# Latent attention's rotary halves exchanged on VectorE, and its queries summed in half a bank

## The chip, the cores and the metric

The kernel runs on one core of one Trainium2 chip. The metric is the device time of one execution in microseconds (us); the figure of a kernel is the median of its runs. TensorE (PE in the profile, PEld for its weight loads) multiplies into PSUM banks of 128 rows by 512 float32 columns; VectorE (DVE) and ScalarE (ACT) read and write PSUM and SBUF; SyncE's queue (SP) issues nearly all transfers.

## The reference

Two layers over 256 tokens of width 2048, all in float32. A layer projects the normed input to differential attention (8 heads), multi-head latent attention (8 heads) and two gates, mixes both attentions through gates, and adds a SwiGLU block and a gated embedding. What matters here is how latent attention makes its queries and its shared key:

```python
qf = (rmsnorm(cq, g_q_latent[i]) @ w_q_up[i]).reshape(b, s, MLA_HEADS, 128 + 64)
q_nope = qf[..., :128]
q_rope = apply_rope(qf[..., 128:], cos_m, sin_m)
k_rope = apply_rope(kr[:, :, None, :], cos_m, sin_m)[:, :, 0, :]
scores = (q_nope . k_nope + q_rope . k_rope) * scale

def apply_rope(x, cos, sin):
    x1, x2 = jnp.split(x, 2, axis=-1)
    return concatenate([x1 * cos - x2 * sin, x2 * cos + x1 * sin])
```

The rotary part has 64 features, and feature d meets feature d + 32 (or d - 32). The latent `cq` has 512 features; the eight heads have 8 x 128 unrotated and 8 x 64 rotated query features. The order of the 64 features within query and key does not matter to the scores, as long as both have the same.

## The kernel before, in words

**Layout.** Activations stand with features on the 128 rows and the 256 tokens on the columns. Every matmul is a float32 product in parts: an operand u is kept as `[hi | lo]`, 512 columns, where `hi` is u rounded to a shorter type (fp32r) and `lo` the rest; a weight tile is split by `piece` into `hi` (ACT, L187) and `lo` (DVE, through the helper of L75) after its transfer by SP (L186). Weights come in pieces of up to eight 128 x 128 tiles; there are four buffers for arriving pieces and three each for `hi` and `lo`.

**A product.** `emit` makes two matmuls for each tile: weight `hi` by all 512 columns of u (L212), and weight `lo` by the 256 `hi` columns, added on the second half of the bank (L216). The result stands in two halves of a bank, and `joined` adds them: ACT copies the second half to SBUF (L242), DVE adds the first. There are four such banks (`ps_mm`). `product` does this for one output tile, `pair` for two tiles that share one piece.

**Latent queries and keys.** `queries_up(n)` takes a pair of tiles of `w_q_up`, each a product over the four tiles of `cq`. For n below 8 the tiles are unrotated queries: `joined`, then `split` into an operand. For n of 8 and 10 they are rotated queries, two heads of 64 features each on the 128 rows: `joined`, then `rotated`. `rotated` multiplies by a permutation matrix in float32 (`swap`, L367) to get each row's partner, and makes a * cos + partner * sin with three DVE instructions. The shared key (64 features, made once per layer by `narrow`) takes the same way with two matrices that also copy it to the other 64 rows: `halves` (L366) and `swaps` (L367). The three matrices and the frequencies come in one constant, `rope_c`, to the tile `rc`. For the differential heads, whose partners are 8 rows apart, `queries_keys` exchanges with `stream_shuffle` (L524), which permutes rows within each group of 32.

**Order.** `pipelined` walks the heads of an attention and between them steps a generator of other products: `beside` gives the differential attention its fill (keys, queries and keys of later heads, then `settle`, which norms the heads done, and the latent queries); the gate products fill the latent attention. The program is written in this order, and a scheduler with its own timing model then settles the order of the instructions on each engine for the whole kernel, except where the code pins it. Each engine works through its queue in order.

Of the kernel before, what the change touches and what calls it, by code (L numbers as in the profile page):

```python
# [16 lines left out]
ALU = mybir.AluOpType  # L17
AX = mybir.AxisListType

P = 128  # L20
T = 256
DM = 2048
NC = DM // P
DEPTH = 2
# [29 lines left out]
def encoder(ctx, tc, x, p, positions, cols, lams, wq, wk, wv, wcq, wckv, wkr, wga, wgb,  # L54
            w_q_up, w_kn, w_v, w_bd, w_bm, w_out, w_gate, w_up, w_down, w_pin, w_pg, rope_c, out):
    nc = tc.nc
    V, A, PE = nc.vector, nc.scalar, nc.tensor
# [10 lines left out]
    def scratch(tag, bufs, n=T):  # L68
        return tmp.tile([P, n], F32, tag=tag, name=tag, bufs=bufs)

    def bank(ps=ps_at, tag="at", name="at", shape=(P, 2 * T)):
        return ps.tile(list(shape), F32, tag=tag, name=name)

    def tt(o, a, b, op):
        return V.tensor_tensor(out=o, in0=a, in1=b, op=op)  # L75

    def stt(o, a, s, b, op0, op1):
        return V.scalar_tensor_tensor(out=o, in0=a, scalar=s, in1=b, op0=op0, op1=op1)
# [14 lines left out]
    def operand(t):  # L93
        return t.rearrange("p c t -> p (c t)")
# [4 lines left out]
    rc = const.tile([P, rope_c.shape[1]], F32, name="rc")  # L99
    nc.scalar.dma_start(gcol, cols)  # L100
    off = {}
    at = 0
# [13 lines left out]
    times = const.tile([P, 6], F32, name="times")  # L116
    for k in range(6):
        nc.gpsimd.memset(times[:, k : k + 1], 64.0 * 0.25 ** (k % 3) * (EPS if k > 2 else 1.0 / DM))
    swap, swaps, halves = (rc[:, 4 + j * P : 4 + (j + 1) * P] for j in range(3))
    aside = [fa(j) for j in range(5)]  # L120
    posi = aside[0][:, 0, :].bitcast(I32)
    posf = aside[0][:, 1, :]
# [86 lines left out]
    def emit(acc, hi, lo, at, us, first, last, inside=None):  # L209
        for j, u in enumerate(us):  # L210
            s, start, stop = slice((at + j) * P, (at + j + 1) * P), first and j == 0, last and j == len(us) - 1
            lead = PE.matmul(acc, hi[:, s], u, start=start, stop=False)  # L212
            if inside and inside[0] == j:
                with tc.issue_after(lead.ins):
                    inside[1]()
            rest = PE.matmul(acc[:, T:], lo[:, s], u[:, :T], start=False, stop=stop)  # L216
            if inside and inside[0] == j:
                tc.keep_in_program_order(rest)
# [9 lines left out]
            emit(acc, hi, lo, 0, us[a : a + m], a == 0, a + m == n, inside and (inside[0] - a, inside[1]))  # L228
        return acc

    def pair(src, us):

        n = len(us)
        hi, lo = piece(src.rearrange("n p m -> p n m"), 2 * n)
        for j in range(2):
            acc = bank(ps_mm, "mm", "mm")
            emit(acc, hi, lo, j * n, us, True, True)
            yield acc

    def joined(acc, o=None):  # L240
        t = scratch("join", 3)
        A.activation(t, acc[:, T:], AF.Copy)  # L242
        o = scratch("a", 4) if o is None else o
        tt(o, acc[:, :T], t, ALU.add)
        return o

    def split(u, src, gain=None):
        hi, lo = u[:, :T], u[:, T:]
        if gain is None:
            return A.activation(hi, src, AF.Copy), tt(lo, src, hi.bitcast(F32), ALU.subtract)  # L250
        return A.activation(hi, src, AF.Copy, scale=gain), stt(lo, src, gain, hi.bitcast(F32), ALU.mult, ALU.subtract)
# [91 lines left out]
    def stream(us, gain):  # L343

        acc = squares()

        def add(c):
            split(us[c], xT[:, c, :], g(gain, c))
            square_into(acc, xT[:, c, :], c == 0)

        return acc, add
# [9 lines left out]
        nc.gpsimd.memset(t.bitcast(F32), 0.0)  # L361

    def rotated(a, c_, s_, o=None):
        r = bank()
        if o is None:
            PE.matmul(r[:, T:], halves, a, start=True, stop=True)  # L366
        PE.matmul(r[:, :T], swap if o is not None else swaps, a, start=True, stop=True)  # L367
        t = scratch("sh", 2)
        tt(t, r[:, :T], s_, ALU.mult)
        tt(a, a if o is not None else r[:, T:], c_, ALU.mult)  # L370
        tt(a, a, t, ALU.add)
        if o is None:
            for j, t in enumerate(krs):
                split(t[64 * j : 64 * j + 64], a[64 * j : 64 * j + 64])
        else:
            split(o, a)
# [59 lines left out]
        return tmp.tile([P, 2, T], dt, tag=tag, name=tag, bufs=2)  # L436

    last_exp = [None]
    ROPE16 = [(j + 8) if j < 8 else (j - 8) if j < 16 else j for j in range(32)]

    def values(src, us, load=None):
# [43 lines left out]
    for L in range(DEPTH):  # L485

        steps = values(wv[L], ua, None if L else load)
        for vd in steps:
            if L == 0 and vd is not None:
# [3 lines left out]
                with after_splits():  # L493
# [5 lines left out]
                    cos_p, sin_p, cos_m, sin_m = tables()  # L499
# [20 lines left out]
        def queries_keys(h, *inside):  # L520
            for which, w in enumerate((wq, wk)):
                a = joined(product(w[L, h], ua, inside=(8, inside[which]) if inside else None))
                sh = scratch("sh", 2)
                V.stream_shuffle(sh, a, ROPE16)  # L524
                tt(sh, sh, sr, ALU.mult)
# [5 lines left out]
        cq, ckv = ub[8:12], ub[12:14]  # L531
        qn, kn, qr = [], [], ub[14:]
# [17 lines left out]
                split(kn[-1], joined(acc))  # L550

        def queries_up(n):
            for acc in pair(w_q_up[L, n : n + 2], cq):
                if n < MH:
                    qn.append(operand(fa(len(qn), F32R)))
                    split(qn[-1], joined(acc))
                else:
                    if n > MH:
                        qr.append(operand(fc(len(qr) - 2, F32R)))
                    at = qr[len(qr) - 1] if n > MH else qr[ropes[0]]  # L560
                    rotated(joined(acc), cos_m, sin_m, at)
                    ropes[0] += 1

        ropes = [0]
# [144 lines left out]
        acc, add = stream(ub, f"g_ffn{L}")  # L709
# [11 lines left out]
        for part, (f0, f1) in enumerate(FF_PARTS):  # L721
            for f in range(f0, f1):
                a = pre.pop(0) if pre else joined(product(w_gate[L, f], ub))
                tt(a, a, R, ALU.mult)
                s = scratch("sig", 2)
# [7 lines left out]
            if last:  # L733
                acc, add = stream(ub, f"g_ple{L}")
# [12 lines left out]
        if final:  # L747
            acc = squares()
# [5 lines left out]
        else:  # L754
            acc, add = stream(ua, f"g_mix{L + 1}")
        for n in range(NC - 2 * final):
            a = pre.pop(0) if pre else joined(product(w_pg[L, n], ub))
            tt(a, a, R, ALU.mult)
            s = scratch("sig", 2)
# [18 lines left out]
    for n in ends:  # L778
        parts[n] = [piece(w_pg[L, n][:, a * P : (a + PT) * P], PT) for a in (0, PT)]
        m = banks[n, 0] = bank(ps_mm, "mm", "mm")  # L780
# [7 lines left out]
    for n in ends:  # L788
        m = banks[n, 1] = bank(ps_mm, "mm", "mm")
        for j in range(whole[n], NC):  # L790
            w = slice(j % PT * P, (j % PT + 1) * P)
# [94 lines left out]
        ("g_q_latent0", 4), ("g_q_latent1", 4), ("g_kv_latent0", 2), ("g_kv_latent1", 2), ("g_subln", 2)]  # L886


def rope_constants():


    c = np.zeros((P, 4 + 3 * P), np.float32)
    f32 = np.float32
    for base, dim in ((0, 16), (2, 64)):
        inv = f32(THETA) ** (-np.arange(0, dim, 2, dtype=f32) / f32(dim))
        for q in range(P):
            d = q % 64
            if d < dim:
                c[q, base] = inv[d % (dim // 2)]
                c[q, base + 1] = -1.0 if d < dim // 2 else 1.0  # L900
    for q in range(P):
        c[q, 4 + (q ^ 32)] = 1.0
        for m in (q, q ^ 64):
            c[q, 4 + P + (m ^ 32)] = 1.0
            c[q, 4 + 2 * P + m] = 1.0
    return c


def tiles(w):

    d, k, n = w.shape
    w = w.reshape(d, k // P, P, n // P, P).transpose(0, 3, 2, 1, 4)
    return np.ascontiguousarray(w).reshape(d, n // P, P, k)
# [13 lines left out]
def laid_out(a):  # L927
    a = {k: np.asarray(v) for k, v in a.items()}
    w_in = a["w_in"]
    cut = np.cumsum([0, 1024, 1024, 1024, QR, KVR, 64, DM, DM])  # L930
    z = [w_in[:, :, cut[j] : cut[j + 1]] for j in range(8)]
    up = a["w_q_up"].reshape(DEPTH, QR, MH, 192)
    kv = a["w_kv_up"].reshape(DEPTH, KVR, MH, 256)
    flat = lambda w: w.reshape(w.shape[0], w.shape[1], -1)
    named = {f"{n}{i}": a[n][i] for n in ("g_mix", "g_ffn", "g_ple", "g_q_latent", "g_kv_latent") for i in range(DEPTH)}
    named["g_final"] = a["g_final"]
    named["g_subln"] = a["g_subln"]
    return {
        "x": np.ascontiguousarray(a["x"][0].T.reshape(NC, P, T).transpose(1, 0, 2)),
        "p": np.ascontiguousarray(a["p"][:, 0].transpose(0, 2, 1).reshape(DEPTH, 2, P, T).transpose(0, 2, 1, 3)),  # L940
        "positions": np.ascontiguousarray(a["positions"]),
        "cols": np.ascontiguousarray(np.concatenate([columns(named[n]) for n, _ in COLS], axis=1)),
        "lams": np.ascontiguousarray(np.stack([a["lambda_q1"], a["lambda_q2"], a["lambda_k1"], a["lambda_k2"]], axis=1).reshape(1, -1)),
        "wq": tiles(z[0]), "wk": tiles(z[1]), "wv": wide(z[2]), "wcq": tiles(z[3]), "wckv": tiles(z[4]),
        "wkr": np.ascontiguousarray(z[5].reshape(DEPTH, NC, P, 64).transpose(0, 2, 1, 3)).reshape(DEPTH, P, NC * 64), "wga": tiles(z[6]), "wgb": tiles(z[7]),
        "w_q_up": tiles(np.concatenate([flat(up[..., :128]), flat(up[..., 128:])], axis=2)),
        "w_kn": tiles(flat(kv[..., :128])), "w_v": wide(flat(kv[..., 128:])),
        "w_bd": tiles(a["w_branch_diff"]), "w_bm": tiles(a["w_branch_mla"]), "w_out": tiles(a["w_out"]),
        "w_gate": tiles(a["w_gate_up"][:, :, :DFF]), "w_up": tiles(a["w_gate_up"][:, :, DFF:]),
        "w_down": tiles(a["w_down"]), "w_pin": tiles(a["w_ple_in"]), "w_pg": tiles(a["w_ple_gate"]),  # L950
        "rope_c": rope_constants(),
    }
# [17 lines left out]
```

## Time and profile before

| | us |
|---|---|
| median of 3 runs | 2838.72 |
| lowest, highest | 2837.63, 2839.24 |
| the profiled execution | 2838.84 |
| its span in the profile | 2837.0 |

The granted TensorE clock was 0.999 of full speed over the span. Busy shares of the span: PE 100%, weight loads 88%, DVE 73%, ACT 54%. Durations of single matmuls in the profile overlap one another, so the distance between the starts of neighbours is the measure of what one costs. In rows of groups, `x` is the count and the two numbers behind the bar are busy us and mean ns; behind the second bar stands the idle time of the engine before them and what ended it. Tiles carry the program's names: `a` is a joined result, `at` a bank of the second pool, `mm` one of `ps_mm`, `sh` a scratch tile of the rotation. DVE's instructions are listed under the helpers L75 (two tensors), L78 and L81.

### The profile page before, as it was taken

Reading aid. Unit: us, or ns where it says so; the run is one execution under the profiler, and the core shown is the slowest. Engines: PE = TensorE matmul, PEld = TensorE weight load, DVE = VectorE, ACT = ScalarE, POOL = GpSimd, SP = SyncE. Lnnn points to the kernel's source line nnn. Section 1 sums busy time; section 2 is a strip of 40 time slices with the busy share of each in tenths; the row PEclk is TensorE's granted clock in tenths of the full one; section 3 lists DMA queues with packets and bytes.
Section 4 is the critical chain, followed back from the end, with each engine's and each line's share of the span. In section 5 each row is a group of like instructions: output and inputs, shape, how many; then the busy total and the mean of one; then the engine's idle time right before and its main releaser. Section 6 shows DMA issues by size and latency. Waiting matters only on the chain.

```text
span 2837.0 us, 44038 instructions
## 1 busy us (share of the span) xinstructions
PE 2826.8 (100%) x16743; PEld 2498.5 (88%) x16743; DVE 2073.0 (73%) x3537; ACT 1527.5 (54%) x2548; POOL 1.9 (0%) x15
## 2 busy tenths in 40 slices
PE   9999999999999999999999999999999999999998
PEld 7888888888888888888888888888888888888888
DVE  7997658776666766677869976687766666666777
ACT  6676545554444444455646755555544444444556
POOL 0000000000000000000000000000000000000000
PEclk9999999999999999999999999999999999999999
DMA  7544466666665566566665445666666656666664
GB/s 244 169 161 149 162 194 197 192 194 193 187 199 193 182 198 201 194 193 194 193 192 169 155 150 168 195 197 194 193 193 187 199 193 187 202 194 194 193 193 155
DMA packets 156596, 531.49 MB, mean 187 GB/s; under 512 B 16992, under 2 KB 24160, under 8 KB 156384
## 3 DMA queue, kind: packets, MB, share of 16 engines
q1 hardware_dynamic: 155952, 528.09, 58.9%
q8 instruction: 131, 2.15, 0.3%
q14 instruction: 81, 0.66, 0.1%
q10 hardware_dynamic: 432, 0.59, 0.1%
HBM read 526.52 MB, written 2.10 MB: 186 GB/s over the span
## 4 chain that ended last, share of the span: by engine, by line
PE 99%; DMA 1%; DVE 0%; ACT 0%; issue 0%; SPq 0%; DVEq 0%; ACTq 0%
PE mm L212 61%; PE mm L216 31%; PE S L406 1%; PE mmv L462 1%; PE mmv L460 1%; PE mmv L461 1%; DMA w<-in_wv 1%; PE at L424 1%; PE at L632 1%; PE at L689 0%; PE mm L776 0%; PE mm L392 0%; DVE wlo L75 0%; PE at L647 0%; DVE a L75 0%; PE at L367 0%
## 5 line engine op out<-in xcount | busy, mean ns | idle before, releaser
L187 ACT ACTIVATE whi<-w 128x1024 fp32r<-128x1024 f32 (+2 forms) x1030 | 1063.1, 1033 | 1241.4 <-issue 704.3
L75 DVE TENSOR_TENSOR wlo<-w,whi 128x1024 fp32r<-128x1024 f32 (+2 forms) x1030 | 1224.4, 1189 | 676.5 <-ACT whi L187 667.8
L212 PE MATMUL mm<-ub,whi 128*128 128x512 f32 x3936 | 1342.3, 390 | 0.3
L212 PE MATMUL mm<-ua,whi 128*128 128x512 f32 x3712 | 1271.4, 390 | 0.0
L216 PE MATMUL mm<-ub,wlo 128*128 128x256 f32 x3936 | 1085.1, 276 | 0.0
L216 PE MATMUL mm<-ua,wlo 128*128 128x256 f32 x3712 | 1027.3, 277 | 0.0
L212 PEld LDWEIGHTS mm<-ub,whi 128*128 128x128 f32 x3936 | 738.2, 188 | 153.1 <-DVE a L75 0.7
L212 PEld LDWEIGHTS mm<-ua,whi 128*128 128x128 f32 x3712 | 696.0, 188 | 142.0
L216 PEld LDWEIGHTS mm<-ub,wlo 128*128 128x128 f32 x3936 | 738.8, 188 | 1.1
L216 PEld LDWEIGHTS mm<-ua,wlo 128*128 128x128 f32 x3712 | 696.9, 188 | 2.4 <-DVE wlo L75 0.6
L75 DVE TENSOR_TENSOR a<-mm,join 128x256 f32<-128x256 f32 (+1 forms) x423 | 175.1, 416 | 1.6 <-ACT join L805 1.4
L242 ACT ACTIVATE join<-mm 128x256 f32<-128x256 f32 x452 | 166.5, 370 | 5.2 <-PE mm L216 4.8
L75 DVE TENSOR_TENSOR xT<-xT,mm 128x256 f32<-128x256 f32 x256 | 106.8, 420 | 41.5 <-PE mm L216 37.7
L75 DVE TENSOR_TENSOR a<-a,row 128x256 f32<-128x256 f32 (+1 forms) x209 | 87.5, 422 | 5.9
L75 DVE TENSOR_TENSOR a<-a 128x256 f32<-128x256 f32 x120 | 50.8, 425 | 4.0
L460 PE MATMUL mmv<-whi,ua 128*128 128x512 f32 x128 | 50.1, 395 | 1.7 <-ACT whi L187 1.7
L75 DVE TENSOR_TENSOR ua<-a,ua 128x256 fp32r<-128x256 f32 x120 | 49.9, 417 | 1.0 <-ACT ua L250 1.0
L461 PE MATMUL mmv<-whi,ua 128*128 128x512 f32 x128 | 49.6, 391 | 0.0
L250 ACT ACTIVATE ua<-a 128x256 fp32r<-128x256 f32 x120 | 48.2, 403 | 2.6 <-DVE a L75 2.6
L415 ACT ACTIVATE E<-S,nm 128x256 f32<-128x256 f32 x96 | 44.2, 472 | 2.1 <-DVE nm L81 2.0
L462 PE MATMUL mmv<-wlo,ua 128*128 128x512 f32 x128 | 43.8, 393 | 0.1
L75 DVE TENSOR_TENSOR ssq<-ssq,sq 128x256 f32<-128x256 f32 x96 | 40.1, 417 | 0.3 <-ACT sq L280 0.3
(195 smaller groups left out, 1209.8 us busy)
## 6 DMA issues: line engine op xcount, KB each, us to landing
w<-in_w_gate SPq DMA_DIRECT2D x176, 512.0 KB, 4.7
w<-in_w_up SPq DMA_DIRECT2D x176, 512.0 KB, 4.7
w<-in_w_down SPq DMA_DIRECT2D x128, 512.0 KB, 4.1
w<-in_wga SPq DMA_DIRECT2D x64, 512.0 KB, 3.8
w<-in_wgb SPq DMA_DIRECT2D x64, 512.0 KB, 4.1
w<-in_w_out SPq DMA_DIRECT2D x64, 512.0 KB, 4.6
w<-in_w_pg SPq DMA_DIRECT2D x64, 512.0 KB, 4.7
w<-in_w_down SPq DMA_DIRECT2D x64, 384.0 KB, 3.7
```

Source lines behind the costliest of these rows:

```text
L75: return V.tensor_tensor(out=o, in0=a, in1=b, op=op)
L187: last_split[:] = A.activation(hi[:, :m], w[:, :m], AF.Copy), tt(lo[:, :m], w[:, :m], hi[:, :m].bitcast(F32), ALU.subtract)
L212: lead = PE.matmul(acc, hi[:, s], u, start=start, stop=False)
L216: rest = PE.matmul(acc[:, T:], lo[:, s], u[:, :T], start=False, stop=stop)
L242: A.activation(t, acc[:, T:], AF.Copy)
L250: return A.activation(hi, src, AF.Copy), tt(lo, src, hi.bitcast(F32), ALU.subtract)
L406: PE.matmul(S[:, b, :], q[:, b * P : (b + 1) * P], k, start=j == 0, stop=j == len(pairs) - 1)
L415: last_exp[0] = A.activation(E[:, b, :], S[:, b, :], AF.Exp, bias=nm[:, b : b + 1], scale=scale, accum_out=sm[:, b : b + 1])
L424: PE.transpose(tp[:, kb, b * P : (b + 1) * P], W[:, b, kb * P : (kb + 1) * P], ident)
L460: PE.matmul(banks[half][b], xh, hi[:, s], start=a + j == 0, stop=False)
L461: PE.matmul(banks[half][b], xl, hi[:, s], start=False, stop=False)
L462: last_mm[:] = [PE.matmul(banks[half][b], xh, lo[:, s], start=False, stop=a + j == n - 1)]
```

## The change

Three things change together.

1. In `rotated` the partner comes from `stream_shuffle` with the list `SWAP16`, which exchanges the two halves of 16 rows in each group of 32. For this the 64 rotary features are stored in another order (`LATENT_ORDER`), in which partners stand 16 rows apart in one group of 32: the columns of the shared key's weights and of `w_q_up`'s rotary part are reordered when the arrays are laid out, and the frequency and sign columns with them. For the queries the shuffle and the cosine product read the accumulator's bank itself. The key keeps its product with `halves` and loses the one with `swaps`.
2. `queries_up` calls `pair` with `one=True`: for each tile of `cq` there are three matmuls of 256 columns, `hi` by u's `lo`, `hi` by u's `hi` and `lo` by u's `hi`, all added on the first 256 columns of the bank, so the sum stands there whole, and `joined` is not called.
3. `rc` holds one matrix instead of three: 132 columns instead of 388.

```diff
-    swap, swaps, halves = (rc[:, 4 + j * P : 4 + (j + 1) * P] for j in range(3))
+    halves = rc[:, 4 : 4 + P]
...
-    def pair(src, us):
+    def pair(src, us, one=False):
         n = len(us)
         hi, lo = piece(src.rearrange("n p m -> p n m"), 2 * n)
         for j in range(2):
             acc = bank(ps_mm, "mm", "mm")
-            emit(acc, hi, lo, j * n, us, True, True)
+            if one:
+                acc = acc[:, :T]
+                for k, u in enumerate(us):
+                    s = slice((j * n + k) * P, (j * n + k + 1) * P)
+                    for i, (w, x_) in enumerate(((hi, u[:, T:]), (hi, u[:, :T]), (lo, u[:, :T]))):
+                        PE.matmul(acc, w[:, s], x_, start=k + i == 0, stop=k + i == n + 1)
+            else:
+                emit(acc, hi, lo, j * n, us, True, True)
             yield acc
...
     def rotated(a, c_, s_, o=None):
-        r = bank()
         if o is None:
-            PE.matmul(r[:, T:], halves, a, start=True, stop=True)
-        PE.matmul(r[:, :T], swap if o is not None else swaps, a, start=True, stop=True)
+            r = bank()[:, :T]
+            PE.matmul(r, halves, a, start=True, stop=True)
+        else:
+            r, a = a, scratch("a", 4)
         t = scratch("sh", 2)
-        tt(t, r[:, :T], s_, ALU.mult)
-        tt(a, a if o is not None else r[:, T:], c_, ALU.mult)
+        V.stream_shuffle(t, r, SWAP16)
+        tt(t, t, s_, ALU.mult)
+        tt(a, r, c_, ALU.mult)
         tt(a, a, t, ALU.add)
...
+    SWAP16 = [(j + 16) % 32 for j in range(32)]
...
         def queries_up(n):
-            for acc in pair(w_q_up[L, n : n + 2], cq):
+            for acc in pair(w_q_up[L, n : n + 2], cq, True):
                 if n < MH:
                     qn.append(operand(fa(len(qn), F32R)))
-                    split(qn[-1], joined(acc))
+                    split(qn[-1], acc)
...
-                    rotated(joined(acc), cos_m, sin_m, at)
+                    rotated(acc, cos_m, sin_m, at)
...
+LATENT_ORDER = [q // 32 * 16 + q % 16 + q % 32 // 16 * 32 for q in range(64)]
...
-    c = np.zeros((P, 4 + 3 * P), np.float32)
+    c = np.zeros((P, 4 + P), np.float32)
...
-            d = q % 64
+            d = q % 64 if dim < 64 else LATENT_ORDER[q % 64]
```

More of the change, by code (lines that the diff above doesn't have):

```diff
@@ L901, in rope_constants @@
     for q in range(P):
-        c[q, 4 + (q ^ 32)] = 1.0
         for m in (q, q ^ 64):
-            c[q, 4 + P + (m ^ 32)] = 1.0
-            c[q, 4 + 2 * P + m] = 1.0
+            c[q, 4 + m] = 1.0
     return c
@@ L944, in laid_out @@
         "wq": tiles(z[0]), "wk": tiles(z[1]), "wv": wide(z[2]), "wcq": tiles(z[3]), "wckv": tiles(z[4]),
-        "wkr": np.ascontiguousarray(z[5].reshape(DEPTH, NC, P, 64).transpose(0, 2, 1, 3)).reshape(DEPTH, P, NC * 64), "wga": tiles(z[6]), "wgb": tiles(z[7]),
-        "w_q_up": tiles(np.concatenate([flat(up[..., :128]), flat(up[..., 128:])], axis=2)),
+        "wkr": np.ascontiguousarray(z[5][:, :, LATENT_ORDER].reshape(DEPTH, NC, P, 64).transpose(0, 2, 1, 3)).reshape(DEPTH, P, NC * 64), "wga": tiles(z[6]), "wgb": tiles(z[7]),
+        "w_q_up": tiles(np.concatenate([flat(up[..., :128]), flat(up[..., 128:][..., LATENT_ORDER])], axis=2)),
         "w_kn": tiles(flat(kv[..., :128])), "w_v": wide(flat(kv[..., 128:])),
```

## The prediction

> **What bounds the kernel now.** I read the page first, then the waits of PE, then busy time by stretches around the stage that the change touches, and last the matmuls of that stage in order of time.
>
> ```profile
> span 2837.0 us, 44038 instructions
> PE 2826.8 (100%) x16743; PEld 2498.5 (88%) x16743; DVE 2073.0 (73%) x3537; ACT 1527.5 (54%) x2548; POOL 1.9 (0%) x15
> PE 99%; DMA 1%; DVE 0%; ACT 0%; issue 0%; SPq 0%; DVEq 0%; ACTq 0%
> ```
>
> Of the chain that ended last, 99% is matmul work. The waits of PE, the next view, have two rows in all:
>
> ```profile
> PE mmv L460 <- ACT whi L187: 1.7, 1, 1.7
> PE at L476 <- DVE ones L115: 1.0, 1, 1.0
> ```
>
> Both lie in the first 25 us. So TensorE's queue sets the end, and an edit pays what it takes out of that queue, less what it puts in, as long as no new wait opens. Where one could open is seen in the stretches (columns: length, then busy PE, PEld, DVE, ACT, POOL). The latent queries are made from about 200 to 230 us in the first layer; the third row is the stage behind it.
>
> ```profile
> 201.00:209.00 8.00, 8.00 (x50) 7.06 (x48) 7.80 (x20) 8.00 (x27) 0.00 (x0) 1.00 0.51 166
> 217.00:232.00 15.00, 14.85 (x99) 13.38 (x98) 14.07 (x37) 12.12 (x34) 0.00 (x0) 1.00 0.35 112
> 232.00:333.00 101.00, 101.00 (x633) 90.71 (x632) 68.53 (x139) 59.01 (x118) 0.00 (x0) 1.00 0.47 151
> ```
>
> PE is full, but here DVE is full too (7.80 of 8.00, 14.07 of 15.00), which it is not behind it (68.53 of 101). An edit that adds to DVE here could stall PE; one that relieves it can't hurt by that.
>
> **Removed from PE: the exchange by a matmul.** L367 is `rotated`'s product with a permutation matrix; each call is two instructions.
>
> ```profile
> L367 PE MATMUL at<-a,rc x20: 377/378/382, 192.1 to 1636.2; 128*128 128x256 f32 x20
> L366 PE MATMUL at<-a,rc x4: 377/378/378, 191.7 to 1600.1; 128*128 128x256 f32 x4
> ```
>
> So there are ten calls in both layers: eight for the queries, two for the shared key, whose other product (L366, `halves`, two calls) stays. A matmul's duration overlaps its neighbours' here, so I price by the distance between starts:
>
> ```profile
> 191.69 0.59 PE L366 MATMUL at<-a,rc 128*128 128x256 f32 x2
> 192.12 0.59 PE L367 MATMUL at<-a,rc 128*128 128x256 f32 x2
> 192.55 0.60 PE L424 MATMUL at<-ident,E 128*128 128x128 f32 x4
> 213.16 0.60 PE L367 MATMUL at<-a,rc 128*128 128x256 f32 x2
> 213.41 0.58 PE L212 MATMUL mm<-ub,whi 128*128 128x512 f32 x1
> 213.83 0.28 PE L216 MATMUL mm<-ub,wlo 128*128 128x256 f32 x1
> 300.15 0.39 PE L212 MATMUL mm<-ua,whi 128*128 128x512 f32 x1
> 300.38 0.28 PE L216 MATMUL mm<-ua,wlo 128*128 128x256 f32 x1
> ```
>
> The key's call holds the queue from 192.12 to 192.55, 0.43 us. A query's call and the 512-column matmul behind it take 213.16 to 213.83, 0.67 us; such a matmul alone takes 0.23 (300.15 to 300.38), so the call costs 0.44. Eight by 0.44 and two by 0.43 are **4.38 us off PE**.
>
> **Added to PE: a third matmul for each tile of the latent queries.** Twelve loads bring their weights:
>
> ```profile
> L186 SPq DMA_DIRECT2D w<-in_w_q_up x12: 367/368/379, 185.1 to 1608.2; - x12
> ```
>
> Each feeds two accumulators, 24 in all, of four tiles each: 96 steps. A step was one matmul of 512 columns and one of 256; it becomes three of 256, each with its own weight load. Both sorts stand back to back in the latent attention's stage:
>
> ```profile
> 304.24 0.39 PE L212 MATMUL mm<-ua,whi 128*128 128x512 f32 x1
> 304.46 0.28 PE L216 MATMUL mm<-ua,wlo 128*128 128x256 f32 x1
> 304.57 0.52 PE L406 MATMUL S<-fb,fa 128*128 128x256 f32 x3
> 304.93 0.52 PE L406 MATMUL S<-kr,fc 128*128 128x256 f32 x3
> 305.29 0.52 PE L406 MATMUL S<-fb,fa 128*128 128x256 f32 x3
> 305.65 0.52 PE L406 MATMUL S<-kr,fc 128*128 128x256 f32 x3
> 306.01 0.60 PE L424 MATMUL at<-ident,E 128*128 128x128 f32 x4
> ```
>
> From 300.15 to 304.57 lie 13 pairs (first and last are quoted), 0.340 us each. The twelve score matmuls take 304.57 to 306.01, 1.44 us, 0.120 each; three are 0.360. So a step grows by 0.020 us, and 96 steps put **1.92 us on PE**. The other end: a 256-column matmul right behind a 512-column one takes 0.11 (304.46 to 304.57), and three of these are no longer than the pair, so nothing is added. I take 1.92, because the score rows are a run of 256-column matmuls with a load each, just what the queries become. The Trainium skill, TensorE: Matmul & The Clock Gate, section Back-to-back issue gap, gives columns over 2.4 GHz plus 2.5 ns; by it a step would grow by 2.5 ns, an estimate of 0.24 us for all 96, and the sum would be 4.1 us instead of 2.5. The trace's 120 ns against that rule's 109 decides for the dearer value.
>
> **DVE and ACT.** The 24 joins go: one ACT copy and one DVE add each. `split` reads the bank instead of SBUF. Each of ten rotations gains a shuffle, whose multiplications stay.
>
> ```profile
> L242 ACT ACTIVATE join<-mm 128x256 f32<-128x256 f32 x452 | 166.5, 370 | 5.2 <-PE mm L216 4.8 <-PE mm L392 0.3
> L75 DVE TENSOR_TENSOR a<-mm,join 128x256 f32<-128x256 f32 x420 | 174.3, 416 | 0.1
> L524 DVE STREAM_SHUFFLE sh<-a 128x256 f32<-128x256 f32 x32 | 14.1, 441 | 0.0
> L75 DVE TENSOR_TENSOR sh<-at,sin_m 128x256 f32<-128x256 f32 x8 | 3.3, 416 | 0.5 <-PE at L367 0.5
> L75 DVE TENSOR_TENSOR a<-a,cos_m 128x256 f32<-128x256 f32 x8 | 3.3, 413 | 0.0
> L75 DVE TENSOR_TENSOR ub<-at,ub 128x256 fp32r<-128x256 f32 x16 | 6.7, 417 | 1.0 <-ACT ub L250 0.7
> L75 DVE TENSOR_TENSOR wlo<-w,whi 128x1024 fp32r<-128x1024 f32 x930 | 1138.6, 1224 | 627.7 <-ACT whi L187 619.3
> ```
>
> Reading a bank costs DVE no more than reading SBUF (416 and 417 ns from `at`, 413 from `a`), so `split` keeps its price, and I give the shuffle its 441 ns. No row has a shuffle out of a bank; it lies between nothing and twice its price, and ten by 0.44 us are 4.4 us of DVE at most. DVE: 24 by 0.416 less ten by 0.441 is 5.6 us off, about 2.8 per layer in the very stage that is full; ACT: 24 by 0.370, 8.9 us off. Both are beside PE and pay nothing directly. New waits: DVE's shuffle and its `lo` subtraction stand in its queue where the join's add stood, behind the same accumulator or its ACT copy; what is queued behind them is the weight split of 1.22 us, for which PE's next product waits. A bank of four is held through the shuffle and two multiplications for rotations, and through one subtraction otherwise. With 2.8 us less in DVE's queue I put this at nothing; the price if the cover goes is the second rival.
>
> **The smaller constants.** `rc` loses 256 of 388 columns.
>
> ```profile
> rc<-in_rope_c SPq DMA_DIRECT2D x1, 194.0 KB, 8.5
> 22.52 0.33 SPq L158 DMA_DIRECT2D rc<-in_rope_c  x1
> 23.72 0.50 PE L460 MATMUL mmv<-whi,ua 128*128 128x512 f32 x1 [1.68 <-ACT whi L187]
> ```
>
> It is issued at 22.52, after the transfer that PE's last early wait hangs on, so 128 KB less pays nothing; at most it pays the 1.7 us of that wait, if the new order put it ahead. Reordering the weights' columns changes no transfer.
>
> **Sum.** 4.38 off, 1.92 on: 2.46 us less. The profiled execution took 2838.84 us, 1.84 beyond its span and 0.12 above the median of 2838.72. From the median: **2836.3 us**. That is 0.09%, where about 0.2% (5.7 us) is what a measurement of this kernel can tell from no change.
>
> **The rivals.** *The third matmul is free.* The runs of 256 columns go at the 0.11 of a pair, 4.38 us off, and DVE's relief closes the gap that PE shows in this stage:
>
> ```profile
> 217.52 0.59 PE L406 MATMUL S<-fb,fa 128*128 128x256 f32 x3
> 218.26 0.50 PE L212 MATMUL mm<-ub,whi 128*128 128x512 f32 x1
> ```
>
> Three matmuls take 0.74 here instead of 0.36, 0.4 us in each layer. Together 5.2 us off: 2833.5. For it: DVE is full there. Against: the score rows. Chance 0.20, and half of it with a little more luck in the order, past the 0.2%.
>
> *Late weight splits, slower.* The order of all queues is worked out anew. If in it the first reader of an accumulator stands ahead of a weight split that is due earlier, DVE waits for PE and PE then for the split: up to 1.22 us for each of the twelve pieces, 14.6 less 2.46, so 2850.9. It is slower by over 0.2% from the seventh piece on ((5.7 + 2.46) / 1.22 = 6.7). For it: DVE has 0.20 us free between 201 and 209. Against: it loses 2.8 us of work per layer, and the join's add stood in the same place. Chance 0.10.
>
> *Weight loads become the bound, slower.* Loads go up by 96 less 20, 76 by 188 ns:
>
> ```profile
> L216 PEld LDWEIGHTS mm<-ub,wlo 128*128 128x128 f32 x3936 | 738.8, 188 | 1.1
> ```
>
> If they lay bare, that is 14.3 us on: 2853.0 with no matmul time saved. The Trainium skill, Perfetto Trace Analysis, section Identifying the Most-Contended Engine, would read TensorE's headroom from the share of LDWEIGHTS, 88% here, and not from that of matmuls. Against: score matmuls start every 0.120 us under loads of 0.188, so loads overlap. Chance 0.03.
>
> *Nothing comes of it.* What PE saves it waits for DVE's and ACT's splits in the full stage: 2838.7, within 1 us. For it: the rows of 201 to 232. Against: DVE and ACT shed more than PE. Chance 0.10.
>
> **Numbers.** The forecast, 2834.5 to 2837.5, has 0.57. Faster by over 0.2% is half the first rival and 0.03 of unknown order: 0.13; slower is the two slow ones: 0.12 (late splits mostly count if many); within 0.2% keeps 0.75. The range reaches down to the free third matmul with its closed gaps, and up over no change by a few late splits: 2833.0 to 2840.0.
>
> **What would show it.** L367 is gone from the matmuls and 96 new ones of 256 columns stand in its place; twelve of them in a row span about 1.44 us; joins fall from 452 to 428; DVE's busy time falls by about 5.6 us and ACT's by 8.9; PE's waits still lie in the first 25 us. New rows of PE waiting for `wlo` or `whi` between 200 and 232 would make it wrong on the slow side; runs of twelve at 1.36 us on the fast side.

## The result, and the profile after

The changed kernel takes 2856.39 us (median of 6 runs, 2854.06 to 2860.80) against 2838.83 (6 runs, 2837.63 to 2839.24): a ratio of 1.0065, interval 1.0052 to 1.0078. It is slower by 17.6 us, where 2.5 us faster was forecast. The profiled execution took 2854.06 us, 15.2 more than the one before.

The page, the lines that answer to those shown of before:

```profile
span 2852.0 us, 44136 instructions
PE 2829.5 (99%) x16819; PEld 2502.2 (88%) x16819; DVE 2070.3 (73%) x3533; ACT 1521.5 (53%) x2524; POOL 1.9 (0%) x15
PE 97%; DVE 2%; DMA 1%; ACT 0%; issue 0%; SPq 0%; DVEq 0%; ACTq 0%
```

PE was 10.2 us of its span idle before (2837.0 less 2826.8) and is now 22.5, and 2% of the chain lies on DVE. Of PE's waits two lie in the first 30 us, as before; the others name the place:

```profile
PE at L657 <- DVE fa L81: 6.2, 2, 3.1
PE at L433 <- DVE E L78: 2.6, 2, 1.3
PE at L657 <- DVE ub L78: 1.7, 2, 0.9
PE at L642 <- ACT wt L435: 1.4, 2, 0.7
PE S L415 <- ACT E L424: 0.8, 2, 0.4
PE mm L242 <- DVE a L75: 0.6, 2, 0.3
```

L657 are the transposes of `settle`, L433 and L642 belong to the last differential head, L415 are scores, L242 the new matmuls. None of these waits existed; each comes twice, once in each layer. Busy time by stretches (length, PE, PEld, DVE, ACT, POOL, clock, DMA share, GB/s), first 222 to 242 us of the kernel before, then of the one after:

```profile
222.00:242.00 20.00, 20.00 (x122) 17.76 (x122) 17.17 (x50) 12.83 (x32) 0.00 (x0) 1.00 0.39 123
```

```profile
222.00:242.00 20.00, 13.69 (x77) 11.24 (x77) 14.05 (x47) 9.94 (x31) 0.00 (x0) 0.91 0.13 42
230.00:235.00 5.00, 1.08 (x7) 0.60 (x5) 4.55 (x23) 1.30 (x6) 0.00 (x0) 0.96 0.01 3
235.00:238.00 3.00, 2.99 (x8) 2.33 (x9) 1.83 (x5) 0.95 (x3) 0.00 (x0) 0.50 0.00 0
1638.00:1660.00 22.00, 15.69 (x79) 12.91 (x78) 14.81 (x50) 10.88 (x33) 0.00 (x0) 0.84 0.11 36
1652.00:1655.00 3.00, 3.00 (x11) 2.40 (x10) 1.50 (x4) 0.91 (x3) 0.00 (x0) 0.58 0.00 0
1638.00:1641.00 3.00, 1.31 (x9) 0.91 (x8) 3.00 (x9) 1.02 (x4) 0.00 (x0) 0.98 0.44 139
1641.00:1643.00 2.00, 2.00 (x11) 2.00 (x10) 0.36 (x2) 0.00 (x0) 0.00 (x0) 0.50 0.37 137
```

PE stands idle for 6.3 us here in either layer. Even the transfers all but stop (DMA share 0.01 from 230 to 235); I read it so that nothing asks for weights while no product runs. Behind the gap the granted clock is 0.50 over 3 us in the first layer and 0.58 over 3 us in the second, which costs an estimated 1.5 and 1.3 us more (the length by what the clock lacks of 1). The last two rows show one more such stretch in the second layer, from 1641 on, which costs at least 1 us. What stood in the way is seen in order of time, first PE, then ACT and DVE:

```profile
229.74 0.52 PE L415 MATMUL S<-kr,ub 128*128 128x256 f32 x3
233.34 0.83 PE L657 MATMUL at<-ident,fa 128*128 128x128 f32 x4 [3.08 <-DVE fa L81]
235.01 0.69 PE L657 MATMUL at<-ident,fa 128*128 128x128 f32 x2 [0.85 <-DVE ub L78]
235.35 0.78 PE L470 MATMUL mmv<-whi,ub 128*128 128x512 f32 x1
235.94 0.63 PE L471 MATMUL mmv<-whi,ub 128*128 128x512 f32 x1
236.36 0.63 PE L472 MATMUL mmv<-wlo,ub 128*128 128x512 f32 x1
236.79 0.63 PE L470 MATMUL mmv<-whi,ub 128*128 128x512 f32 x1
```

```profile
234.18 0.38 ACT L257 ACTIVATE fa<-mm 128x256 fp32r<-128x256 f32 x1
```

```profile
232.91 1.66 DVE L81 TENSOR_SCALAR fa<-fa,ry 128x128 f32<-128x128 f32 x8
234.48 0.48 DVE L78 SCALAR_TENSOR_TENSOR ub<-at,gsub,ub 128x256 fp32r<-128x256 f32 x1
234.87 0.42 DVE L75 TENSOR_TENSOR fa<-mm,fa 128x256 fp32r<-128x256 f32 x1
235.59 0.42 DVE L75 TENSOR_TENSOR fa<-mm,fa 128x256 fp32r<-128x256 f32 x1
236.65 0.42 DVE L75 TENSOR_TENSOR fa<-mm,fa 128x256 fp32r<-128x256 f32 x1
239.64 0.41 DVE L75 TENSOR_TENSOR fa<-mm,fa 128x256 fp32r<-128x256 f32 x1
```

`fa<-mm` is the split of a query tile straight out of its bank. The products of the last four query tiles (heads 4 to 7) ended near 220 us (the row of the chain further below: 217.98 and 2.13 on); their banks are read between 234.2 and 240. Each goes to `fa(4)` to `fa(7)`, and these tiles still hold the outputs `od` of differential heads 4 to 7 until `settle(4)` has scaled (L81) and transposed them. So four accumulators wait in four banks, which is all that `ps_mm` has. The value products (L470) and the gate products, which filled PE's time before, can't start, and PE follows the last head's softmax and `settle(4)` step by step. The first value product of this stage starts at 235.35; in the kernel before it started here:

```profile
224.93 0.39 PE L460 MATMUL mmv<-whi,ub 128*128 128x512 f32 x1
```

The Trainium skill, PSUM — Partial Sum Buffer, section Summary: rules for kernel authors, says to evacuate promptly. The join did that, into a scratch tile; the split into `fa(4)` to `fa(7)` does it from 234.2 on.

### The profile page after: what moved, and what is told of

The parts are those of the page before. It is cut to its first block, busy times and chain, and to the rows that moved or that the text cites. A ratio compares the mean times of both kernels' runs of the same rounds, so it can differ in the third digit from the quotient of the medians.

```text
span 2852.0 us, 44136 instructions
## 1 busy us (share of the span) xinstructions
PE 2829.5 (99%) x16819; PEld 2502.2 (88%) x16819; DVE 2070.3 (73%) x3533; ACT 1521.5 (53%) x2524; POOL 1.9 (0%) x15
## 4 chain that ended last, share of the span: by engine, by line
PE 97%; DVE 2%; DMA 1%; ACT 0%; issue 0%; SPq 0%; DVEq 0%; ACTq 0%
PE mm L212 60%; PE mm L216 30%; PE S L415 1%; PE mmv L472 1%; PE mmv L470 1%; PE mmv L471 1%; PE mm L242 1%; PE at L433 1%; DVE wlo L75 0%; PE at L642 0%; DMA w<-in_wv 0%; PE at L699 0%; PE mm L786 0%; PE mm L401 0%; DVE a L75 0%
## 5 line engine op out<-in xcount | busy, mean ns | idle before, releaser
L212 PE MATMUL mm<-ub,whi 128*128 128x512 f32 x3840 | 1307.0, 389 | 0.0
L216 PE MATMUL mm<-ub,wlo 128*128 128x256 f32 x3840 | 1058.4, 276 | 0.0
L212 PEld LDWEIGHTS mm<-ub,whi 128*128 128x128 f32 x3840 | 720.1, 188 | 149.2
L216 PEld LDWEIGHTS mm<-ub,wlo 128*128 128x128 f32 x3840 | 720.7, 188 | 0.9
L75 DVE TENSOR_TENSOR a<-mm,join 128x256 f32<-128x256 f32 x399 | 166.2, 418 | 1.5 <-ACT join L815 1.4
L249 ACT ACTIVATE join<-mm 128x256 f32<-128x256 f32 x428 | 156.7, 367 | 3.1 <-PE mm L216 2.8
L470 PE MATMUL mmv<-whi,ua 128*128 128x512 f32 x128 | 50.3, 397 | 1.0 <-ACT whi L187 1.0
```

The costliest lines, as they stand in the source:

```text
L470: PE.matmul(banks[half][b], xh, hi[:, s], start=a + j == 0, stop=False)
```

## The experiments

In the expectations H is the theory just told: four banks are held until `settle(4)` has read `fa(4)` to `fa(7)`. Times of before beside them are medians of 2838.3 to 2838.5 on the same chips.

**Copy the four tiles out first.** The changed kernel with

```diff
-    split(qn[-1], acc)
+    split(qn[-1], copied(acc) if n in (4, 6) else acc)   # ACT copy to a scratch tile
```

> Theory H (held banks): in the changed kernel the four unrotated query tiles of heads 4 to 7 are split straight from their banks into fa(4) to fa(7), which settle(4) still reads; so all four ps_mm banks stay full until settle(4) is done, the value products cannot start, and PE stands idle for about 10 us in each layer. Here these four tiles alone are first copied out of the bank by ACT into a scratch tile; all else stays as changed. H expects the loss gone: 2835 to 2838 us, the 2836.3 of the prediction, and no wait of PE for settle's DVE work. Rival M (the 96 third matmuls and their loads cost far more than 20 ns a step) expects it to stay at 2854 to 2860. Rival O (the new order is merely unlucky) has no reason for a return to the sum of the prediction.

Measured: 2835.64 us (11 runs, 2834.33 to 2838.06), ratio to before 0.9992 (0.9983 to 1.0000). The waits of PE, then the same stretch, then the first value product of the stage:

```profile
PE at L491 <- DVE ones L115: 1.1, 1, 1.1
PE mmv L475 <- ACT whi L187: 1.0, 2, 0.7
PE mm L242 <- DVE a L75: 0.7, 2, 0.3
```

```profile
222.00:242.00 20.00, 20.00 (x132) 18.13 (x131) 15.79 (x43) 12.84 (x32) 0.00 (x0) 1.00 0.37 130
```

```profile
220.69 0.39 PE L475 MATMUL mmv<-whi,ub 128*128 128x512 f32 x1
```

All 96 third matmuls and all shuffles are still there, four copies per layer are added, and 20.8 us go. PE is full, and the value products start at 220.69 us instead of 235.35. That rules out matmul and load prices as the cause.

**The held banks alone.** The kernel before, with one edit for two of six calls:

```diff
-    for acc in pair(w_q_up[L, n : n + 2], cq):
+    for acc in pair(w_q_up[L, n : n + 2], cq, n in (4, 6)):
-    split(qn[-1], joined(acc))
+    split(qn[-1], acc if n in (4, 6) else joined(acc))
```

> The kernel before, with one edit: the four query tiles of heads 4 to 7 are made by three matmuls of 256 columns and split straight from their banks into fa(4) to fa(7). Swap products, joins of all other tiles and the constants stay. Theory H (banks held until settle(4) has read fa(4) to fa(7)): this edit alone brings the loss, with PE waiting for settle's DVE work and the value products behind it: 2848 to 2862 us. Rival O (the loss needs the whole change, an unlucky order of everything): within 2 us of 2838.3.

Measured: 2852.79 us (4 runs), ratio 1.0052 (1.0039 to 1.0066). The waits of PE:

```profile
PE at L654 <- DVE fa L81: 8.3, 2, 4.2
PE at L654 <- DVE ub L78: 1.3, 2, 0.6
```

This edit alone brings a loss of 14.3 us, in the same place. The rival of an unlucky order of everything falls. The loss is less than the 20.8 us that the copies took off the changed kernel. PE is idle here for 4.8 us in each of the two stretches, against 6.3 there; the rest of the difference I did not follow.

**Another place for the result, twice.** The changed kernel, with the tiles of heads 4 and 5 going to two new SBUF tiles; room for them was first taken from the spacer tile between the two kinds of split weights, then from small statistics tiles:

```diff
-    qn.append(operand(fa(len(qn), F32R)))
+    qn.append(operand((fq if len(qn) in (4, 5) else fa)(len(qn), F32R)))
-STEP = 48
+STEP = 16          # first run only
```

> The changed kernel, but the query tiles of heads 4 and 5 go to two new SBUF tiles instead of fa(4) and fa(5); no copy is added, heads 6 and 7 are as before (an unused spacer tile is made 32 columns shorter to make room). H: two of the four banks come free at once, which is what the value products need, so most of the loss goes: 2835 to 2843 us. Rival M: 2854 to 2860, since no matmul is different.

Measured: 2886.74 us (5 runs), ratio 1.0175 (1.0161 to 1.0189), far outside what I expected. The settle wait was gone, but matmuls were slower in most of the kernel: 573 in the 100 us from 1000 on, against 591 before. The shorter spacer had moved the `hi` weight tiles 128 bytes nearer to the `lo` tiles.

> Own SBUF tiles for the queries of heads 4 and 5 once more, but the spacer tile keeps its 48 columns; room is made by cutting small statistics tiles from 16 columns to the 8 that they use. H for the time lost in the earlier run (each pair of matmuls took 349 ns instead of 340, from where the weight tiles lie): that is the spacer's doing, so it is gone here, and with two banks free the settle wait is gone too: 2834 to 2840 us. Rival (the new tiles themselves slow the matmuls, or own tiles do not help): 2850 or more.

Measured: 2837.88 us (11 runs), ratio 0.9999 (0.9990 to 1.0008), and PE's longest wait in the stage is

```profile
PE S L415 <- ACT E L424: 1.1, 2, 0.6
```

The two new tiles (`fq`) are filled on DVE as soon as their products end:

```profile
217.67 0.42 DVE L75 TENSOR_TENSOR fq<-mm,fq 128x256 fp32r<-128x256 f32 x1
219.47 0.42 DVE L75 TENSOR_TENSOR fq<-mm,fq 128x256 fp32r<-128x256 f32 x1
```

Without a copy, and with banks free because the destination is free, the loss is gone: it is the destination, not reading the bank without a join, that costs. This is 2 us behind the kernel with copies; the two intervals overlap, and I did not follow it.

**The parts alone.** The shuffle with all joins and pairs kept, and the three matmuls with swap products kept:

```diff
-    for acc in pair(w_q_up[L, n : n + 2], cq, True):     # shuffle only, from the changed kernel
+    for acc in pair(w_q_up[L, n : n + 2], cq):
+    split(qn[-1], joined(acc)) ... rotated(joined(acc), cos_m, sin_m, at)
```

> The exchange by shuffle alone: all query tiles by the pair of 512 and 256 columns with the join, as before the change. H: nothing is held, only the ten swap products leave PE: 2838.8 less 4.4 is 2834.4, between 2833.5 and 2835.5. Rival S (the shuffle in DVE's full queue delays the weight splits): 2845 or more.

Measured: 2837.86 us (11 runs), ratio 0.9997 (0.9989 to 1.0006). A miss: 0.4 us off instead of 4.4, which the interval leaves out (it ends at 3.1). The profile shows new waits in the stage:

```profile
PE mm L212 <- DVE a L75: 3.3, 6, 1.1
```

PE now waits for `a`, the join's add, which frees the bank: six waits of up to 1.1 us that were not there. I read it so that the swap products had been cover for the joins in DVE's full queue: with them PE came later. Over the whole span PE's idle time is up by 1.7 us only (11.9 against 10.2), since a wait at the start is shorter, and its busy time is down by 3.0 instead of 4.4; that difference stays open.

```diff
-    for acc in pair(w_q_up[L, n : n + 2], cq):           # three matmuls only, from the kernel before
+    for acc in pair(w_q_up[L, n : n + 2], cq, True):
+    split(qn[-1], copied(acc)) ... rotated(copied(acc), cos_m, sin_m, at)
```

> The kernel before, with the three matmuls of 256 columns for all 24 query tiles; each is copied out of its half bank by one ACT copy in place of copy and add; the swap products stay. H: only the price of the 96 third matmuls, 1.9 us: 2840.7, between 2839 and 2842. Rival M: 2850 or more.

Measured: 2839.38 us (11 runs), ratio 1.0005 (0.9996 to 1.0013), 1.1 us on where 1.9 was the price; the interval holds both, and no change as well, so the price is bounded and not settled by it.

**Two mixtures.** The changed kernel with the join for all unrotated tiles, and with the join for the last four alone:

```diff
+    for acc in pair(w_q_up[L, n : n + 2], cq, n >= MH):          # unrotated tiles joined
+    for acc in pair(w_q_up[L, n : n + 2], cq, n not in (4, 6)):  # last four joined
```

> The changed kernel, with all unrotated query tiles back to the pair of 512 and 256 columns and the join; the rotated ones stay as changed. H: no bank is held, so no loss: the sum is 4.4 off for the swap products and 32 third matmuls at 20 ns on, 2834.6; less good, up to 2837.5, if DVE's adds free the banks late, as the shuffle alone showed with 3.3 us of PE waiting for the join's add. Rival O: anything, 2850 as well.

> The changed kernel, with only the tiles of heads 4 to 7 back to the pair of 512 and 256 columns and the join. H: the join frees the bank, so no loss; against the kernel with a copy (2835.6) it saves 32 third matmuls at 20 ns, 0.6 us, and adds four DVE adds per layer: 2834.5 to 2836.5. Rival O: no reason to come near that.

Measured: 2836.70 us (11 runs), ratio 0.9994 (0.9985 to 1.0003), and 2835.19 us (11 runs, 2833.83 to 2835.61), ratio 0.9987 (0.9978 to 0.9997). Both are where they were expected. The second, with the join only where the destination is late, is the lowest of all and below both kernels; its interval overlaps that of the kernel with copies.

**The spacer alone.** The kernel before, with one number changed:

```diff
-STEP = 48
+STEP = 16          # or 32
```

> The kernel before with one number changed: the spacer tile between the lo and the hi weight tiles has 16 columns instead of 48, so the hi tiles lie 128 bytes nearer. No work is different. Theory P (the place of the weight tiles sets the pace of the matmul pairs): 2870 to 2890 us, pairs at 349 ns in most of the feed-forward stages. Rival (the slow pairs in the earlier run came from its two new tiles): 2837 to 2840.

> The same with 32 columns, 64 bytes nearer than before. Theory P: the pace depends on the place, so either the fast 340 ns or the slow 349 ns a pair, perhaps something between, 2838 to 2890. The rival: 2837 to 2840.

Measured: 2887.81 us (4 runs), ratio 1.0157 (1.0126 to 1.0188), and 2924.83 us (4 runs), ratio 1.0303 (1.0286 to 1.0321), beyond the 2890 that I expected at most. The miss above is the spacer's. With 16 columns one of the four runs took 2868.60 us and the others 2887 to 2888, at a granted clock of 0.999 to 1.000 in all four.

## Why the prediction was wrong

**The step that failed** is in the part on DVE and ACT: "A bank of four is held ... through one subtraction otherwise. With 2.8 us less in DVE's queue I put this at nothing". I asked how long the readers of the bank take and how full their queue is, not whether the place they write to is free. The join's target was a scratch tile with four buffers; `split`'s target is `fa(4)` to `fa(7)`, whose last reader is `settle(4)`. The prediction named the wait for a bank and priced it by the wrong thing. The one edit alone costs 14.3 us in the kernel before (2852.79 against 2838.45).

**The slow rival** had the right sign and stage, but a wrong mechanism: weight splits delayed in DVE's queue. Between 230 and 235 DVE did work, but on `settle`; no wait of PE for `wlo` between 200 and 242 shows. Its 2850.9 is near the result by accident.

**The sum itself** fits as a whole, its terms alone do not. With only the bank's hold taken away the kernel takes 2835.64, 2.7 us below before, where the sum said 2.46; the interval reaches from nothing to 4.8. In that profile PE is busy for 3.2 us less than before (2823.6 against 2826.8). The terms:

```profile
L242 PE MATMUL mm<-ub,whi 128*128 128x256 f32 x192 | 35.8, 286 | 0.6 <-DVE a L75 0.6
L242 PE MATMUL mm<-ub,wlo 128*128 128x256 f32 x96 | 27.2, 284 | 0.0
L377 DVE STREAM_SHUFFLE sh<-mm 128x256 f32<-128x256 f32 x8 | 3.6, 448 | 0.0
L249 ACT ACTIVATE join<-mm 128x256 f32<-128x256 f32 x428 | 156.7, 367 | 3.1 <-PE mm L216 2.8 <-PE mm L401 0.2
```

288 matmuls of 256 columns replace 96 pairs. In the chain of the changed kernel eighteen of them last

```profile
217.98 2.13 PE mm L242 x18
```

0.118 us each, where I took 0.120. The Trainium skill, TensorE: Matmul & The Clock Gate, section Back-to-back issue gap, gives a formula, by which it would be an estimated 0.109; the page calls that the gap of an isolated matmul. The shuffle out of a bank took 448 ns against the 441 assumed, and joins fell to 428 as said. DVE's and ACT's busy time fell by 2.7 and 6.0 us, not 5.6 and 8.9; part of this is that instructions packed in a queue overlap (0.33 us apart at 0.41 long, at 213.62 and 213.95 of the changed kernel), so that one less takes off less than its duration. The parts alone, 0.4 off and 1.1 on, do not add up to the 2.7 off together, though the intervals are wide. The removed swap products are the term that was off by itself: 0.4 us where 4.38 stood. It would fit that the two parts help each other: the shuffle takes work from PE, and without the adds DVE frees banks in time. That is a reading, not shown. The prediction had DVE's relief as worth nothing directly.

**The account of the profiled execution**: its span is 15.0 us longer (2852.0 against 2837.0). Of this 12.3 is idle time of PE (22.5 against 10.2); the two stretches, with 6.3 each, hold all of it. The other 2.7 is busy time (2829.5 against 2826.8), where the sum would have taken 2.5 off, so 5.2 us of busy time are to be placed. The low clock can account for most of it: 20 us at 0.91 and 22 us at 0.84 are 5.3 us lost, less what fell into PE's idle time.

**The clock** is a loss that no term had. From 229.74 PE issues three score matmuls and then nothing till 233.34, and at 235 the granted clock is 0.50: the value products' 512 columns start 0.43 us apart (236.36 to 236.79), where 0.23 is usual. The Trainium skill, TensorE: Matmul & The Clock Gate, Part 1, says that an idle window of some 3.4 us halves the clock until PE has been busy as long. This trace agrees with the halved clock, but not with so long an idle time: the gap in the waits is 3.1 us, and before the stretch at 1641 PE was busy for 1.3 of 3 us, with waits of 1.3 and 0.4 us. The window runs freely, by that page, so which gaps bring the slow time may differ from run to run. The six runs have a granted clock from 0.998 at 2854 us down to 0.994 at 2860 to 2861.

## What to carry to other kernels

When a step is dropped that moved a result out of a PSUM bank, look for what its scratch tile decoupled: the bank is then held until the final destination is free, and the last reader of that destination may come long after. Count banks against such results; when as many wait as there are banks, TensorE loses its filler work and not only the one product. Drop the copy where the destination is free and keep it where it is not: that mixture had the lowest time here, 0.9987 of the kernel before (0.9978 to 0.9997).

## What the runs showed of the hardware that was not expected

A shift of tiles in SBUF changed the pace of matmuls. The spacer lies between the `lo` and the `hi` tiles; with 48, 16 and 32 columns the kernel before takes 2838.5, 2887.8 and 2924.8 us, with no work changed. Busy time and counts of the same 100 us in the three, in that order:

```profile
1000.00:1100.00 100.00, 100.00 (x591) 88.73 (x590) 65.85 (x99) 46.97 (x65) 0.00 (x0) 1.00 0.66 201
```

```profile
1000.00:1100.00 100.00, 100.00 (x573) 87.95 (x572) 63.87 (x97) 46.62 (x64) 0.00 (x0) 1.00 0.64 191
```

```profile
1000.00:1100.00 100.00, 100.00 (x570) 87.32 (x569) 64.70 (x102) 45.90 (x65) 0.00 (x0) 1.00 0.63 186
```

The clock is full and PE busy in all three, but it gets through 591, 573 and 570 matmuls. The run of 2868.60 shows that the place alone does not fix the time. Whether the `hi` weight tiles are what matters or other tiles that moved with them, and why, stays open. An edit that changes the size of a tile can bring this in unasked, as one experiment here did. The smaller `rc`, 1024 bytes less per row, did not: with it, the kernel with copies has 591 matmuls in these 100 us, as many as before.
